# Gate products in a sequence of their own beside stick-breaking attention, with the adaptive visits gathered

## The chip, the cores and the metric

One core of a Trainium2 chip runs the whole program. The metric is the device time of one execution in microseconds (us). The engines work at the same time, each through its own instructions in order: TensorE (PE) does matrix products, ScalarE (ACT) and VectorE (DVE) work on elements, GpSimd (POOL) mostly issues DMAs here, SyncE (SP) issues the loads. They wait for each other by semaphores.

## The reference

One layer of a streaming encoder, for 1024 prompt rows and 32 sample rows of width 1024. What matters here:

```python
ada = silu(c) @ w_ada + b_ada            # 6 parts of 1024: shift, scale, gate, twice
h = rms_norm(x, g_pre_mix) * (1 + sc1) + sh1
p = h @ w_in                             # split: latents, rope key, SB q, k, v, gate A, gate B
...
# branch B: stick-breaking attention, 8 heads of 64, strictly causal
z = einsum('bqhd,bshd->bhqs', q, k) * SB_SCALE
sp = where(mask, softplus(z), 0.0)
later = cumsum(sp, reverse=True) - sp
a = where(mask, exp(log_sigmoid(z) - later), 0.0)
o_b = einsum('bhqs,bshd->bqhd', a, v)
...
merged = sigmoid(gate A) * (o_A @ w_proj_a) + sigmoid(gate B) * (o_B @ w_proj_b)
```

Then come an output projection, a residual with ada's gate, a convolutional feed-forward part of width 2816 and a second residual.

## The kernel before

The program runs its stages one after the other: `stage_h`, `stage_qkv`, `stage_sb`, `stage_lat`, `stage_mla`, `stage_merge`, `stage_up`, `stage_down`. The change lies in `stage_sb` (about 183 to 520 us of the profiled execution), and in what it calls.

`stage_sb` does the prompt's stick-breaking attention in four passes, one for each pair of heads. Beside it PE does two other things that nothing in the stage needs at once: the products of the two gates (`gates`), and a part of `ada` (`ada_step`).

Within a pass the order of PE, ACT and DVE is written out by hand: `sb_attend` goes through the list `ORDER`, and `manual_schedule` keeps that order on these three engines. SP and POOL are ordered by a scheduler. A token is a letter, then a query block of a head (0 to 7: head and a pair of 128 rows), then the tile or the key block, and a or b where a tile is done in two parts. The letters are:

- S: scores on PE (lines L1154, L1155). a, e, l: ACT takes the absolute value, exp and ln (L742, L744, L746). x: DVE makes softplus of it (L748). c: DVE's scan from the right, which is the cumulative sum (L755, L752); k copies the carry. d: DVE subtracts from the scores (L760). E: ACT takes exp (L762).
- T: PE transposes (L803). h and v: ACT and DVE split the transposed weights into a high and a low part (L68, L71). V: PE multiplies by the values (L817). o and p: ACT and DVE take the result out, and POOL stores it.
- f: one step of the gate products, three matmuls of 128x352 on PE (L75, L76, L77). G: ACT copies a finished gate bank to a "nat" buffer (L1080), and POOL stores it in `gd` (L1081). W and w: ACT and DVE split the next 128 columns of gate weights, which SP has loaded as `wr`, into high and low parts (L68, L71).
- D and Q: DVE adds a partial sum of `ada` (L244), or puts a finished part in place.

A gate tile `m` is 128 columns of `w_in`, done in three blocks of 352 rows and 8 steps each. There are 16 gate tiles, four to a pass. In the generator `steps`, behind the first block of each gate tile, stands a visit to `ada`: the products of two "A" tiles (128 rows of `w_ada` by 1024 columns) with the short matrix `cT`, each as 8 matmuls in the profile (L236); they take two f's of the list. `ada_step` also asks SP for the next two A tiles. So a pass has 96 f's for gates and 8 for ada. `stage_sb` asks for the first two A tiles ahead of the first head's V and of the weights of gate tile 1.

`stage_qkv` ends just before: it spills q, k and v to memory (`spill`, L478, by POOL), from where `queries` and `values` load them.

Of the kernel before, what the change touches and what calls it, by code (L numbers as in the profile page):

```python
# [8 lines left out]
F32 = mybir.dt.float32  # L9
# [35 lines left out]
class K:  # L45
# [182 lines left out]
    def ada_step(self, n, pool, tp, late):  # L228


        nc, a = self.nc, self.a
        ps = self.bank("mm")
        for i, (v, k) in enumerate(self.ada_todo[:n]):
            w = self.ada_w.pop(0)
            for j in range(4):
                nc.tensor.matmul(ps[32 * j : 32 * j + 32, :256], self.cT[:, k], w[:, j * 256 : j * 256 + 256],  # L236
                                 start=i == 0, stop=i == n - 1)
            if i < n - 1:
                yield
        if v > 2 and self.ada_todo[0][1] == 0:  # L240
            self.acc = self.tl(tp, [P, 256], F32, "ada")
            self.ada_bias(v)
        acc = self.acc
        late.append(lambda: nc.vector.tensor_tensor(acc, acc, ps[:, :256], ALU.add))  # L244
        del self.ada_todo[:n]
        self.ada_fetch(n, pool)
        self.ada_sum = v if k == KT - 1 else None
        yield

    def ada_turn(self):  # L250

# [192 lines left out]
    def stage_qkv(self):  # L444
# [245 lines left out]

    ORDER = """
        S0.0 S0.1 a0.0 S1.0 a0.1 e0.0 e0.1 l0.0 f2 l0.1 x0.0 a1.0 x0.1 f1 c0.1 c0.0 e1.0 f1 l1.0 f1 d0.0 d0.1
        E0.0 f1 x1.0 c1.0 E0.1 f1 S1.1 S2.0a a1.1 T0.0 d1.0 f1 G a2.0a h0.0 v0.0 f1 e2.0a f1 e1.1 S2.0b l2.0a D
        f2 l1.1 x2.0a V0.0 E1.0 c2.0a f1 a2.0b o0 f1 x1.1 e2.0b f1 W p0 f1 k2.0a d2.0a l2.0b f1 c1.1 E2.0a f1
        S2.1a x2.0b G f1 a2.1a d1.1 e2.1a c2.0b f2 E1.1 f1 w l2.1a S2.1b f1 a2.1b x2.1a T1.1 e2.1b T1.0 d2.0b
        h1.1 c2.1a f1 h1.0 f1 l2.1b v1.1 S3.0a E2.0b v1.0 f1 a3.0a f1 k2.1a d2.1a G e3.0a x2.1b V1.1 E2.1a c2.1b
# [3 lines left out]
        f2 x3.1b E3.1a f1 x4.0 c3.1b f1 G T3.3 c4.0 S4.1 a4.1 T3.2 h3.3 d3.1b f1 e4.1 v3.3 h3.2 f1 d4.0 f1 l4.1  # L700
        E3.1b v3.2 S5.0 f1 E4.0 x4.1 c4.1 a5.0 V3.3 e5.0 V3.2 l5.0 d4.1 T3.1 E4.1 x5.0 T3.0 h3.1 f1 c5.0 h3.0
        S5.1 S6.0a v3.1 a5.1 f1 v3.0 a6.0a T4.0 e5.1 f1 d5.0 h4.0 V3.1 E5.0 v4.0 f1 l5.1 V3.0 G x5.1 S6.0b e6.0a
        f1 o3 c5.1 f1 a6.0b l6.0a e6.0b f1 p3 l6.0b d5.1 f2 x6.0b E5.1 V4.0 x6.0a f1 o4 c6.0a S6.1a T5.1 p4
        a6.1a T5.0 k6.0a d6.0a h5.1 f1 c6.0b e6.1a f1 G h5.0 v5.1 f1 E6.0a v5.0 S6.1b l6.1a f1 W f1 x6.1a d6.0b
        V5.1 V5.0 D c6.1a E6.0b a6.1b S7.0a w o5 f2 e6.1b l6.1b a7.0a f1 k6.1a p5 e7.0a f1 d6.1a x6.1b E6.1a f1
        c6.1b l7.0a S7.0b f1 x7.0a T6.2 a7.0b f1 d6.1b h6.2 c7.0a f1 E6.1b f1 G e7.0b S7.1a v6.2 f1 k7.0a d7.0a
        l7.0b T6.1 T6.0 a7.1a h6.1 V6.2 x7.0b c7.0b h6.0 S7.1b e7.1a f1 v6.1 E7.0a f1 v6.0 l7.1a f1 d7.0b a7.1b
        f1 x7.1a V6.1 E7.0b V6.0 e7.1b c7.1a f1 G o6 l7.1b f1 p6 k7.1a d7.1a x7.1b f2 E7.1a f1 c7.1b f2 T7.3
        d7.1b T7.2 h7.3 f1 h7.2 E7.1b v7.3 f1 G f1 v7.2 f1 V7.3 V7.2 D T7.1 f1 h7.1 v7.1 T7.0 f1 h7.0 v7.0 f1
        V7.1 f2 V7.0 f1 o7 f1 W p7 f1 Q f1 w G f7 G  # L710
    """.split()

    def sb_attend(self, score, V, out, fill, then):
        nc = self.nc
        act, vec = nc.scalar.activation, nc.vector
        tiles, banks, seen = {}, {}, {}
        common = self.sums(V, out, tiles)
        todo = None
        for x in self.ORDER:
            if todo:  # L720
                todo()
            todo = then.get(x)
            k, x = x[0], x[1:]
            if k in "fGDQWw":
                for _ in range(int(x or 1)):
                    fill(k)
                continue
            h, u = divmod(int(x[0]), 4)
            if k in "SaelxckdE":
                n, i, part = x[0], int(x[2]), x[3:]  # L730
                w = (2 * u + i + 1) * P
                m = w // 2 if part else w
                c0 = m if part == "a" else 0
                if k == "S":
                    if part != "b":
                        tiles[x[:3]] = self.tl(self.At, [P, TP], F32, "A")
                    banks[x] = self.tl(self.ps, [P, 512], F32, "s")
                    score(h, banks[x], 2 * u + i, c0, max(m, 256))
                    continue
                ps, A = banks[x][:, :m], tiles[x[:3]][:, c0 : c0 + m]  # L740
                if k == "a":
                    act(A, ps, AF.Abs)  # L742
                elif k == "e":
                    act(A, A, AF.Exp, scale=-1.0)  # L744
                elif k == "l":
                    act(A, A, AF.Ln, bias=1.0)  # L746
                elif k == "x":
                    vec.scalar_tensor_tensor(A, ps, 0.0, A, ALU.max, ALU.add)  # L748
                elif k == "c":
                    r = A[:, ::-1]  # L750
                    if part == "b":
                        vec.tensor_tensor_scan(r, r, r, seen[x[:3]], ALU.add, ALU.bypass)  # L752
                    else:

                        vec.tensor_tensor_scan(r, self.reset[:, 512 - m : 512][:, ::-1], r, -NEG, ALU.mult, ALU.add)  # L755
                elif k == "k":
                    seen[x[:3]] = self.tl(self.sm, [P, 1], F32, "mn")
                    vec.tensor_copy(seen[x[:3]], A[:, 0:1])
                elif k == "d":
                    vec.tensor_tensor(A, ps, A, ALU.subtract)  # L760
                else:
                    act(A, A, AF.Exp)  # L762
                continue
            common(k, x, h, u)
# [278 lines left out]
    def gates(self):  # L1043
# [3 lines left out]
        w, ps, ada = [self.w_in_tile(2208)], [], []  # L1047
# [3 lines left out]
        def steps():  # L1051
            for m in range(16):
                wh, wl = w.pop(0)
                for b, (c0, n) in enumerate(self.BLK):
                    if b == 0:
                        c = 2208 + (m + 1) * P if m < 15 else 3 * P
                        raw.append(self.wload([(0, 1024, self.a["w_in"][0, :, c : c + P].rearrange("(k p) c -> p k c", p=P), 8)]))
                    ps.append((m, c0, n, self.bank("mm")))
                    for k in range(KT):
                        self.mm3(ps[-1][3][:, :n], wh[:, k], wl[:, k], self.Hh[k][:, c0 : c0 + n],  # L1060
                                 self.Hl[k][:, c0 : c0 + n], k == 0, k == KT - 1)
                        if k < KT - 1:
                            yield
                    if b == 1 and self.ada_sum is not None:
                        ada.append(self.ada_turn())
                    yield
                    if b == 0:
                        yield from self.ada_step(2, self.sm2, self.Sp, ada)
                        if m == 15:
                            self.sample_load(1)  # L1070

        step = steps()

        def do(kind):
            if kind == "f":
                next(step)
            elif kind == "G":
                m, c0, n, x = ps.pop(0)
                g = self.tl(self.At, [P, 512], F32, "nat")
                nc.scalar.copy(g[:, :n], x[:, :n])  # L1080
                nc.gpsimd.dma_start(self.gd[m, :, c0 : c0 + n], g[:, :n])  # L1081
# [24 lines left out]
    def stage_sb(self):  # L1106
# [35 lines left out]
            self.tl(S, [P, TP], F32, "A")  # L1142
        first(0)
        self.sm2 = self.tc.alloc_tile_pool(name="att", bufs=2, reuse_waits="tile")

        self.sent = self.wlast
        queries(0, 0)
        self.ada_w = []
        self.ada_fetch(2, S)
        values(0, 0)  # L1150

        def score(h, ps, i, c0, n):
# [2 lines left out]
            nc.tensor.matmul(ps[:, :n], Q[h][:, q], self.KLz[h][:, c0 : c0 + n], start=False, stop=True)  # L1155
# [1451 lines left out]
```

## Time and profile before

| | us |
|---|---|
| median of 3 runs (1705.19 to 1708.30) | 1707.84 |
| the profiled execution | 1706.82 |
| its span | 1704.7 |
| first score of pass 1 on PE | 193.01 |
| first score of pass 2 | 278.65 |
| first score of pass 3 | 358.06 |
| first score of pass 4 | 437.46 |

The granted clock of PE over the span is 0.994. In a row of a timeline stand the start in us from the span's start, the length in us, the engine, line and operation, the tile written and the tiles read, and the number of instructions; in square brackets is the engine's idle time ahead of it, with what released it. A matmul's start is exact, its end is modelled, so the start of the next one tells how long it held PE. In the table by stretches the brackets hold the number of instructions.

### The profile page before, as it was taken

The numbers are of one execution on the slowest core, as the hardware profiler recorded it, in microseconds if no ns is written. First come the engines' busy times: TensorE is split into PE (matmuls) and PEld (weight loads), VectorE is DVE, ScalarE is ACT, GpSimd is POOL, SyncE is SP. The second block draws the span as 40 slices with busy tenths as digits, with TensorE's granted clock in tenths as the row PEclk, the third lists the DMA queues.
The fourth block names the chain that finished last, engine by engine and source line by source line (L and its number), as shares of the span: only waits on it lengthen the run. The fifth ranks groups of instructions, "written<-read, shape, count | busy, mean of one in ns | idle before, by whom it ended". The sixth has DMA issues, their size and how long they took to land. (4 is left out here: it accounts for less than half of the span.)

```text
span 1704.7 us, 30268 instructions
## 1 busy us (share of the span) xinstructions
PE 1660.8 (97%) x11646; PEld 1512.1 (89%) x11646; DVE 1272.9 (75%) x2129; ACT 993.6 (58%) x1945; POOL 292.8 (17%) x569
## 2 busy tenths in 40 slices
PE   5999999999999999999999999999999999999997
PEld 3999889999999898998889789999999999887885
DVE  4865697979783688777766779887787777787456
ACT  4544597978774667777763476444444444544442
POOL 3113311111110221111100221221121111110013
PEclk8999999999999999999999999999999999999999
DMA  9345984647432421222374531433333333697643
GB/s 333 100 133 180 280 250 130 200 117 227 150 104 66 149 79 47 67 68 70 107 238 140 173 131 62 134 104 131 131 104 132 131 108 133 231 331 250 207 139 120
DMA packets 185728, 255.20 MB, mean 150 GB/s; under 512 B 14702, under 2 KB 125056, under 8 KB 185584
## 3 DMA queue, kind: packets, MB, share of 16 engines
q1 hardware_dynamic: 164944, 194.11, 36.5%
q0 software_dynamic: 20416, 59.08, 9.8%
q8 instruction: 91, 1.49, 0.4%
q14 instruction: 53, 0.43, 0.1%
q10 hardware_dynamic: 224, 0.09, 0.0%
HBM read 187.86 MB, written 64.57 MB: 148 GB/s over the span
## 5 line engine op out<-in xcount | busy, mean ns | idle before, releaser
L68 ACT ACTIVATE wh<-wr 128x1024 fp32r<-128x1024 f32 (+5 forms) x163 | 132.2, 820 | 226.3 <-PE s L2061 80.4
L71 DVE TENSOR_TENSOR wl<-wr,wh 128x1024 fp32r<-128x1024 f32 (+5 forms) x163 | 149.9, 928 | 78.0 <-ACT wh L68 77.6
L75 PE MATMUL mm<-hh,wh 128*128 128x352 f32 x456 | 153.0, 336 | 0.0
L76 PE MATMUL mm<-hl,wh 128*128 128x352 f32 x456 | 149.5, 328 | 0.4 <-DVE hl L331 0.3
L77 PE MATMUL mm<-hh,wl 128*128 128x352 f32 x456 | 148.7, 326 | 0.0
L2060 PE MATMUL mm<-T,wh 128*128 128x256 f32 (+1 forms) x376 | 108.1, 288 | 0.0
L2062 PE MATMUL mm<-T,wl 128*128 128x256 f32 (+1 forms) x376 | 107.0, 285 | 0.3 <-DVE wl L71 0.2
L2061 PE MATMUL mm<-T,wh 128*128 128x256 f32 (+1 forms) x376 | 106.7, 284 | 0.0
L2060 PE MATMUL s<-T,wh 128*128 128x256 f32 (+1 forms) x348 | 99.2, 285 | 0.0
L2062 PE MATMUL s<-T,wl 128*128 128x256 f32 (+1 forms) x348 | 99.1, 285 | 0.0
L2061 PE MATMUL s<-T,wh 128*128 128x256 f32 (+1 forms) x348 | 99.0, 284 | 0.0
L71 DVE TENSOR_TENSOR wl<-S,wh 128x1024 fp32r<-128x1024 f32 (+1 forms) x55 | 59.1, 1077 | 49.2 <-ACT wh L68 48.8
L76 PEld LDWEIGHTS mm<-hl,wh 128*128 128x128 f32 x456 | 86.4, 190 | 3.3 <-DVE hl L331 1.8
L75 PEld LDWEIGHTS mm<-hh,wh 128*128 128x128 f32 x456 | 86.4, 190 | 3.2 <-ACT A L762 1.6
L2201 DVE SCALAR_TENSOR_TENSOR u<-u,c,u 128x1058 f32<-128x1058 f32 x68 | 87.0, 1316 | 2.0 <-ACT u L2198 0.7
L77 PEld LDWEIGHTS mm<-hh,wl 128*128 128x128 f32 x456 | 86.5, 190 | 0.2
L803 PE MATMUL tr<-c,A 128*128 128x128 f32 x576 | 84.2, 275 | 0.9 <-DVE A L919 0.3
L68 ACT ACTIVATE wh<-S 128x1024 fp32r<-128x1024 f32 (+1 forms) x55 | 51.8, 943 | 49.5 <-PE s L2061 13.4
L2062 PE MATMUL tr<-T,wl 128*128 128x272 f32 (+1 forms) x272 | 77.6, 285 | 0.2 <-DVE wl L71 0.2
L2060 PE MATMUL tr<-T,wh 128*128 128x272 f32 (+1 forms) x272 | 77.7, 286 | 0.0
L2061 PE MATMUL tr<-T,wh 128*128 128x272 f32 (+1 forms) x272 | 77.3, 284 | 0.0
L71 DVE TENSOR_TENSOR PTl<-tr,PTh 128x512 fp32r<-128x512 f32 x96 | 64.5, 683 | 13.1 <-ACT PTh L68 12.3
(760 smaller groups left out, 5789.2 us busy)
## 6 DMA issues: line engine op xcount, KB each, us to landing
wr<-in_w_up_dram SPq DMA_DIRECT2D x44, 512.0 KB, 4.0
dr<-in_w_down_dram SPq DMA_DIRECT2D x43, 512.0 KB, 5.9
wr<-in_w_in_dram SPq DMA_DIRECT2D x33, 512.0 KB, 5.4
A<-in_w_ada_dram SPq DMA_DIRECT2D x32, 512.0 KB, 7.6
wr<-gdn SPq DMA_DIRECT2D x30, 512.0 KB, 5.0
gdn<-u POOLq DMA_DIRECT2D x23, 512.0 KB, 5.1
gd<-nat POOLq DMA_DIRECT2D x48, 176.0 KB, 4.1
t<-gd SPq DMA_DIRECT2D x16, 528.0 KB, 5.6
```

The costliest lines, as they stand in the source:

```text
L68: self.nc.scalar.activation(out, in_, AF.Identity, scale=scale)
L71: return self.nc.vector.tensor_tensor(out, full, hi.bitcast(F32), ALU.subtract)
L75: m(ps, lh, rh, start=start, stop=False)
L76: m(ps, lh, rl, start=False, stop=False)
L77: self.pe = m(ps, ll, rh, start=False, stop=stop).ins
L803: self.nc.tensor.transpose(tr[:, (2 * s + q) * P : (2 * s + q + 1) * P], at[q][:, b * P : b * P + P], self.idt)
L2060: m(ps[:, :n], w[0][:, k], x[0][:, k, c], start=first and k == 0, stop=False, skip_group_check=True)
L2061: m(ps[:, :n], w[0][:, k], x[1][:, k, c], start=False, stop=False, skip_group_check=True)
L2062: i = m(ps[:, :n], w[1][:, k], x[0][:, k, c], start=False, stop=k == 3, skip_group_check=True)
L2201: nc.vector.scalar_tensor_tensor(y, u[:, w : w + YW], self.cvT[:, w, cc : cc + 1], y, ALU.mult, ALU.add)
```

## The change

The gate work becomes a sequence of its own. `ORDER` keeps only f, 96 in a pass, at the places where gate steps stood; its other tokens stay as they are. G, W, w, D and Q move to a second list, `GATES`, which ties each to the number of the f behind which it comes, and which is gone through once for each pass. A new letter A in it is a visit of four A tiles, at f32 and f80 of a pass, in place of two tiles for each gate tile. `fill(LEAD)` does the first five f's ahead of the first pass, so ahead of its first scores; from there on every f of `ORDER` is the one five further along in `GATES`, and the last nine f's of the fourth pass find only four steps left.

The first four A tiles are loaded behind the second head's V of the first pass and lie in the pool `sm2`, whose buffers "big" and "A" are taken at once.

```diff
+LEAD = 5
...
     def ada_step(self, n, pool, tp, late):
                 nc.tensor.matmul(ps[32 * j : 32 * j + 32, :256], self.cT[:, k], w[:, j * 256 : j * 256 + 256],
                                  start=i == 0, stop=i == n - 1)
-            if i < n - 1:
-                yield
...
-        yield
...
     ORDER = """
         S0.0 S0.1 a0.0 S1.0 a0.1 e0.0 e0.1 l0.0 f2 l0.1 x0.0 a1.0 x0.1 f1 c0.1 c0.0 e1.0 f1 l1.0 f1 d0.0 d0.1
-        E0.0 f1 x1.0 c1.0 E0.1 f1 S1.1 S2.0a a1.1 T0.0 d1.0 f1 G a2.0a h0.0 v0.0 f1 e2.0a f1 e1.1 S2.0b l2.0a D
-        f2 l1.1 x2.0a V0.0 E1.0 c2.0a f1 a2.0b o0 f1 x1.1 e2.0b f1 W p0 f1 k2.0a d2.0a l2.0b f1 c1.1 E2.0a f1
-        S2.1a x2.0b G f1 a2.1a d1.1 e2.1a c2.0b f2 E1.1 f1 w l2.1a S2.1b f1 a2.1b x2.1a T1.1 e2.1b T1.0 d2.0b
...
-        l3.0a S3.0b V1.0 x3.0a a3.0b o1 f1 p1 T2.2 h2.2 e3.0b d2.1b f1 c3.0a f1 E2.1b f1 l3.0b v2.2 S3.1a k3.0a
-        d3.0a T2.1 h2.1 a3.1a x3.0b E3.0a V2.2 f1 c3.0b T2.0 e3.1a S3.1b h2.0 f1 v2.1 l3.1a f1 G v2.0 a3.1b f1
-        x3.1a W f1 d3.0b V2.1 c3.1a D V2.0 f1 w o2 S4.0 e3.1b E3.0b f1 a4.0 f1 l3.1b f1 p2 e4.0 k3.1a d3.1a l4.0
...
-        f1 o3 c5.1 f1 a6.0b l6.0a e6.0b f1 p3 l6.0b d5.1 f2 x6.0b E5.1 V4.0 x6.0a f1 o4 c6.0a S6.1a T5.1 p4
...
-        V7.1 f2 V7.0 f1 o7 f1 W p7 f1 Q f1 w G f7 G
+        E0.0 f1 x1.0 c1.0 E0.1 f1 S1.1 S2.0a a1.1 T0.0 d1.0 f1 a2.0a h0.0 v0.0 e2.0a e1.1 S2.0b l2.0a f2 l1.1
+        x2.0a V0.0 E1.0 c2.0a f1 a2.0b o0 f1 x1.1 e2.0b f1 p0 f1 k2.0a d2.0a l2.0b f1 c1.1 E2.0a f1 S2.1a x2.0b
+        f1 a2.1a d1.1 e2.1a c2.0b f2 E1.1 f1 l2.1a S2.1b f1 a2.1b x2.1a T1.1 e2.1b T1.0 d2.0b h1.1 c2.1a f1 h1.0
...
+        x3.0a a3.0b o1 f1 p1 T2.2 h2.2 e3.0b d2.1b f1 c3.0a f1 E2.1b f1 l3.0b v2.2 S3.1a k3.0a d3.0a T2.1 h2.1
+        a3.1a x3.0b E3.0a V2.2 f1 c3.0b T2.0 e3.1a S3.1b h2.0 f1 v2.1 l3.1a f1 v2.0 a3.1b x3.1a d3.0b V2.1 c3.1a
...
+        p3 l6.0b d5.1 f2 x6.0b E5.1 V4.0 x6.0a f1 o4 c6.0a S6.1a T5.1 p4 a6.1a T5.0 k6.0a d6.0a h5.1 f1 c6.0b
...
+        T7.1 f1 h7.1 v7.1 T7.0 f1 h7.0 v7.0 f1 V7.1 f2 V7.0 f1 o7 f1 p7 f9
+    """.split()
+
+    GATES = """
+        f9 G f4 W f4 G f3 w f5 G f7 A G f4 W f1 D f1 w f3 G f8 G f8 G W f1 w f8 G f7 G f7 A G f5 D f2 W f2 G w Q f7 G
     """.split()
...
     def gates(self):
                     yield
-                    if b == 0:
-                        yield from self.ada_step(2, self.sm2, self.Sp, ada)
-                        if m == 15:
-                            self.sample_load(1)
...
+            elif kind == "A":
+                self.ada_step(4, self.sm2, self.Sp, ada)
+                if not self.ada_todo:
+                    self.sample_load(1)
...
-        return do
+        parts = [[]]
+        for x in self.GATES * 4:
+            for _ in range(int(x[1:] or 1)):
+                if x[0] == "f":
+                    parts.append([])
+                parts[-1].append(x[0])
+        del parts[0]
+
+        def fill(n=1):
+            for _ in range(n):
+                for k in parts.pop(0) if parts else ():
+                    do(k)
+
+        return fill
...
     def stage_sb(self):
         self.sm2 = self.tc.alloc_tile_pool(name="att", bufs=2, reuse_waits="tile")
+        for g, w, n in (("big", BIG, 3), ("A", TP, 2)):
+            for _ in range(n):
+                self.tl(self.sm2, [P, w], F32, g)
...
         queries(0, 0)
-        self.ada_w = []
-        self.ada_fetch(2, S)
+        self.ada_w, self.ada_sum = [], None
         values(0, 0)
...
         fill = self.gates()
+        fill(LEAD)
         for p in range(4):
             then = {"S2.0a": lambda: queries(p, 1), "S2.1a": lambda: values(p, 1)}
+            if p == 0:
+                then["S2.1a"] = lambda: (values(p, 1), self.ada_fetch(4, self.sm2))
```

More of the change, by code (lines that the diff above doesn't have):

```diff
@@ L692 @@
         S0.0 S0.1 a0.0 S1.0 a0.1 e0.0 e0.1 l0.0 f2 l0.1 x0.0 a1.0 x0.1 f1 c0.1 c0.0 e1.0 f1 l1.0 f1 d0.0 d0.1
-        E0.0 f1 x1.0 c1.0 E0.1 f1 S1.1 S2.0a a1.1 T0.0 d1.0 f1 G a2.0a h0.0 v0.0 f1 e2.0a f1 e1.1 S2.0b l2.0a D
-        f2 l1.1 x2.0a V0.0 E1.0 c2.0a f1 a2.0b o0 f1 x1.1 e2.0b f1 W p0 f1 k2.0a d2.0a l2.0b f1 c1.1 E2.0a f1
-        S2.1a x2.0b G f1 a2.1a d1.1 e2.1a c2.0b f2 E1.1 f1 w l2.1a S2.1b f1 a2.1b x2.1a T1.1 e2.1b T1.0 d2.0b
-        h1.1 c2.1a f1 h1.0 f1 l2.1b v1.1 S3.0a E2.0b v1.0 f1 a3.0a f1 k2.1a d2.1a G e3.0a x2.1b V1.1 E2.1a c2.1b
@@ L702 @@
-        S5.1 S6.0a v3.1 a5.1 f1 v3.0 a6.0a T4.0 e5.1 f1 d5.0 h4.0 V3.1 E5.0 v4.0 f1 l5.1 V3.0 G x5.1 S6.0b e6.0a
-        f1 o3 c5.1 f1 a6.0b l6.0a e6.0b f1 p3 l6.0b d5.1 f2 x6.0b E5.1 V4.0 x6.0a f1 o4 c6.0a S6.1a T5.1 p4
-        a6.1a T5.0 k6.0a d6.0a h5.1 f1 c6.0b e6.1a f1 G h5.0 v5.1 f1 E6.0a v5.0 S6.1b l6.1a f1 W f1 x6.1a d6.0b
-        V5.1 V5.0 D c6.1a E6.0b a6.1b S7.0a w o5 f2 e6.1b l6.1b a7.0a f1 k6.1a p5 e7.0a f1 d6.1a x6.1b E6.1a f1
-        c6.1b l7.0a S7.0b f1 x7.0a T6.2 a7.0b f1 d6.1b h6.2 c7.0a f1 E6.1b f1 G e7.0b S7.1a v6.2 f1 k7.0a d7.0a
@@ new lines @@
+        f1 a2.1a d1.1 e2.1a c2.0b f2 E1.1 f1 l2.1a S2.1b f1 a2.1b x2.1a T1.1 e2.1b T1.0 d2.0b h1.1 c2.1a f1 h1.0
+        f1 l2.1b v1.1 S3.0a E2.0b v1.0 f1 a3.0a f1 k2.1a d2.1a e3.0a x2.1b V1.1 E2.1a c2.1b l3.0a S3.0b V1.0
+        x3.0a a3.0b o1 f1 p1 T2.2 h2.2 e3.0b d2.1b f1 c3.0a f1 E2.1b f1 l3.0b v2.2 S3.1a k3.0a d3.0a T2.1 h2.1
+        a3.1a x3.0b E3.0a V2.2 f1 c3.0b T2.0 e3.1a S3.1b h2.0 f1 v2.1 l3.1a f1 v2.0 a3.1b x3.1a d3.0b V2.1 c3.1a
+        V2.0 f1 o2 S4.0 e3.1b E3.0b f1 a4.0 f1 l3.1b f1 p2 e4.0 k3.1a d3.1a l4.0 f2 x3.1b E3.1a f1 x4.0 c3.1b f1
@@ new lines @@
+        T3.3 c4.0 S4.1 a4.1 T3.2 h3.3 d3.1b f1 e4.1 v3.3 h3.2 f1 d4.0 f1 l4.1 E3.1b v3.2 S5.0 f1 E4.0 x4.1 c4.1
+        a5.0 V3.3 e5.0 V3.2 l5.0 d4.1 T3.1 E4.1 x5.0 T3.0 h3.1 f1 c5.0 h3.0 S5.1 S6.0a v3.1 a5.1 f1 v3.0 a6.0a
+        T4.0 e5.1 f1 d5.0 h4.0 V3.1 E5.0 v4.0 f1 l5.1 V3.0 x5.1 S6.0b e6.0a f1 o3 c5.1 f1 a6.0b l6.0a e6.0b f1
+        p3 l6.0b d5.1 f2 x6.0b E5.1 V4.0 x6.0a f1 o4 c6.0a S6.1a T5.1 p4 a6.1a T5.0 k6.0a d6.0a h5.1 f1 c6.0b
+        e6.1a f1 h5.0 v5.1 E6.0a v5.0 S6.1b l6.1a f1 x6.1a d6.0b V5.1 V5.0 c6.1a E6.0b a6.1b S7.0a o5 f2 e6.1b
@@ new lines @@
+        l6.1b a7.0a f1 k6.1a p5 e7.0a f1 d6.1a x6.1b E6.1a f1 c6.1b l7.0a S7.0b f1 x7.0a T6.2 a7.0b f1 d6.1b
+        h6.2 c7.0a f1 E6.1b f1 e7.0b S7.1a v6.2 f1 k7.0a d7.0a l7.0b T6.1 T6.0 a7.1a h6.1 V6.2 x7.0b c7.0b h6.0
+        S7.1b e7.1a f1 v6.1 E7.0a f1 v6.0 l7.1a f1 d7.0b a7.1b f1 x7.1a V6.1 E7.0b V6.0 e7.1b c7.1a f1 o6 l7.1b
+        f1 p6 k7.1a d7.1a x7.1b f2 E7.1a f1 c7.1b f2 T7.3 d7.1b T7.2 h7.3 f1 h7.2 E7.1b v7.3 f1 v7.2 V7.3 V7.2
+        T7.1 f1 h7.1 v7.1 T7.0 f1 h7.0 v7.0 f1 V7.1 f2 V7.0 f1 o7 f1 p7 f9
@@ L723, in sb_attend @@
             k, x = x[0], x[1:]
-            if k in "fGDQWw":
+            if k == "f":
                 for _ in range(int(x or 1)):
-                    fill(k)
+                    fill()
                 continue
```

5 lines of the change are left out of this document (removed).

## The prediction, on record before the changed kernel ran

> **What bounds the kernel now.** I read the page first, then the table by stretches of 10 us over the stage that the change touches (about 183 to 520 us), then the timelines of each engine at its start and in its second pass.
>
> ```profile
> span 1704.7 us, 30268 instructions
> ...
> PE 1660.8 (97%) x11646; PEld 1512.1 (89%) x11646; DVE 1272.9 (75%) x2129; ACT 993.6 (58%) x1945; POOL 292.8 (17%) x569
> ```
>
> Over the program TensorE (PE) is full and VectorE (DVE) is not. By stretches it looks otherwise (columns: length, then busy time of PE, weight load, DVE, ScalarE (ACT), GpSimd (POOL), granted clock, DMA share, GB/s).
>
> ```profile
> 200.00:210.00 10.00, 10.00 (x63) 8.66 (x64) 6.89 (x13) 5.56 (x14) 4.84 (x10) 0.83 1.07 324
> ...
> 290.00:300.00 10.00, 9.66 (x65) 9.36 (x64) 9.93 (x17) 9.40 (x22) 1.26 (x4) 1.00 0.15 45
> 300.00:310.00 10.00, 10.00 (x76) 8.89 (x76) 9.90 (x18) 8.75 (x19) 1.54 (x3) 1.00 0.55 143
> ...
> 350.00:360.00 10.00, 10.00 (x68) 9.97 (x68) 2.85 (x6) 4.03 (x11) 3.67 (x7) 1.00 0.57 166
> ```
>
> In the middle of a pass (290 to 310) DVE is busy 9.9 of 10 us with the attention's own list; gate products fill PE. At a pass's end (350 to 360) DVE is nearly idle and PE alone sets the time. So in the middle, PE time saved is given back as waiting, while a delay of an ACT or DVE step that the list needs is kept. The first 20 us are a third regime: stalls, and 10 x (1 - 0.83) = 1.7 us of PE time lost to the clock.
>
> **The start of the stage.** PE's rows:
>
> ```profile
> 193.01 0.36 PE L1154 MATMUL s<-KH,Q 128*128 128x256 f32 x1
> ...
> 196.96 0.32 PE L76 MATMUL mm<-hl,wh 128*128 128x352 f32 x1
> 197.12 0.32 PE L77 MATMUL mm<-hh,wl 128*128 128x352 f32 x1
> 199.94 0.64 PE L1154 MATMUL s<-KH,Q 128*128 128x512 f32 x1 [2.49 <-DVE A L760]
> ...
> 201.34 0.85 PE L803 MATMUL tr<-c,A 128*128 128x128 f32 x3
> ...
> 202.99 1.29 PE L236 MATMUL mm<-A,cT 128*32 128x256 f32 x16
> ...
> 212.71 0.44 PE L1154 MATMUL s<-KH,Q 128*128 128x384 f32 x1 [1.36 <-DVE A L760]
> ```
>
> A matmul of a gate step starts 0.16 us after the one before (196.96, 197.12), so a step f of three is 0.48 us, and the five put ahead of the scores are 2.4 us. ACT's rows:
>
> ```profile
> 195.86 0.53 ACT L742 ACTIVATE A<-s 128x128 f32<-128x128 f32 x2
> ...
> 198.36 0.52 ACT L746 ACTIVATE A<-A 128x384 f32<-128x384 f32 x1
> 199.82 0.75 ACT L762 ACTIVATE A<-A 128x128 f32<-128x128 f32 x2 [0.94 <-DVE A L760]
> ...
> 203.10 0.45 ACT L1080 COPY nat<-mm 128x352 f32<-128x352 f32 x1 [0.44 <-PE mm L77]
> ...
> 210.12 1.06 ACT L68 ACTIVATE wh<-wr 128x1024 fp32r<-128x1024 f32 x1 [2.59 <-DMA wr<-in_w_in_dram]
> ...
> 217.15 0.46 ACT L1080 COPY nat<-mm 128x352 f32<-128x352 f32 x1
> ```
>
> *The lead.* ACT takes up the first scores only at 195.86, so scores that start at 193.01 + 2.4 = 195.4 hold it up by 0.2 at most. The lead's 2.4 us fall into the idle 2.49 ahead of 199.94: the second tile's score comes 0.25 earlier at most, not 2.49. What the lead earns is paid at the far end of the stage, where PE alone sets the time: of the last nine f's only four have work. **-2.4**.
>
> *The first weights.* The 2.59 that ACT waits for wr at 210.12, and the 1.36 on PE behind it, go: the two adaptive tiles (1 MB) no longer stand ahead of this load on SP's queue; their loads follow the second head's V instead. **-1.36**. The visit of 1.29 at 202.99, with 0.2 around it, goes from here: **-1.5**.
>
> *Two copies come too early.* GATES ties a gate tile's copy G (ACT) to the number of the f, and the lead moves the first, f9, from behind the first transposes to between e1.0 and l1.0, the row 198.36. The copy writes a "nat" buffer, whose memory was the source of the previous stage's spill qh<-T; the built program has the copy wait for that DMA. GpSimd's rows, and from the table of DMA issues the time to landing:
>
> ```profile
> 196.12 0.56 POOL L478 DMA_DIRECT2D qh<-T  x1 [1.53 <-ACT A L742]
> ...
> 208.11 0.57 POOL L1081 DMA_DIRECT2D gd<-nat  x1
> ```
>
> ```profile
> qh<-T POOLq DMA_DIRECT2D x1, 512.0 KB, 6.5
> ```
>
> ```profile
> gd<-nat POOLq DMA_DIRECT2D x1, 176.0 KB, 8.9
> ```
>
> The spill lands at 196.12 + 6.5 = 202.6; in before the copy ran at 203.10 and never felt it. Now ACT would stand at it from 198.4 to about 202.6, and ACT works in order: l1.0, E0.0, E0.1, a1.1, W, h0.0 queue behind. E0 (199.82 before) ends near 204, T0.0 near 204.3 in place of 201.34: **+3.0**, and PE, out of work at about 200.9, idles some 3.4 us. Bounds: 0 if the spill lands early (1 MB less in the queues) to +3.5. The clock loss of 1.7 then falls behind this gap instead of behind the 2.49: 0, or -1.7 if the gap shrinks. The third copy (f25) needs the first one's buffer back (two "nat" buffers). The first gd DMA is issued at 208.11, behind eight small bias loads on GpSimd's queue which the change leaves ahead of it, and lands at 217.0; before's third copy is at 217.15, just behind. Now ACT reaches it ahead of l2.1a, near 212.5: it waits 0 to 4.5. I take **+1.6**, since an earlier first copy can pull the issue forward by some of it, and DVE stood idle 2 us thereabouts. Start: -0.25 - 1.36 - 1.5 + 3.0 + 1.6 = **+1.5**, from -3.5 (T0.0 0.4 earlier, no waits) to +5.
>
> The Trainium skill, "TensorE: Matmul & The Clock Gate", Part 1, has the clock halve after an idle window of about 3.4 us; here 2.49 us of idle was enough for the stretch at 0.83, so the trace does not bear out that length. By that rule a gap of 3.4 stands at the edge; if it costs nothing, the sum is 1.7 lower.
>
> **A steady pass.** PE's rows of visits, then the steps around the moved ones:
>
> ```profile
> 284.25 0.32 PE L77 MATMUL mm<-hh,wl 128*128 128x352 f32 x1
> 284.50 1.07 PE L236 MATMUL mm<-A,cT 128*32 128x256 f32 x16
> 285.50 0.42 PE L1154 MATMUL s<-KH,Q 128*128 128x320 f32 x1
> 285.75 0.31 PE L1155 MATMUL s<-KL,Q 128*128 128x320 f32 x1
> ...
> 326.03 0.64 PE L236 MATMUL mm<-A,cT 128*32 128x256 f32 x8
> 326.60 0.44 PE L1154 MATMUL s<-KH,Q 128*128 128x384 f32 x1
> ```
>
> A visit of 16 matmuls lasts 1.00 (284.50 to 285.50), of 8 0.57: 0.43 per 8, so 0.14 of each is fixed. Going in costs 0.25 - 0.16 = 0.09, and the first product after it starts the next 0.25 later where about 0.15 would do, 0.1 more: 0.33 per visit. Before: four sites of two tiles a pass, one split by a score, so 20 visits; after: 8 of four tiles (1.00 + 0.86 + 0.2 = 2.05 each). PE saves 12 x 0.33 = 4.0 in all.
>
> ```profile
> 301.71 0.60 ACT L68 ACTIVATE PTh<-tr 128x512 fp32r<-128x512 f32 x1 [0.50 <-PE tr L803]
> ...
> 304.14 0.64 ACT L746 ACTIVATE A<-A 128x512 f32<-128x512 f32 x1
> ...
> 305.50 1.07 ACT L68 ACTIVATE wh<-wr 128x1024 fp32r<-128x1024 f32 x1
> ```
>
> ```profile
> 305.13 0.68 DVE L748 SCALAR_TENSOR_TENSOR A<-s,A 128x512 f32<-128x512 f32 x1
> ...
> 307.39 0.39 DVE L244 TENSOR_TENSOR ada<-ada,mm 128x256 f32<-128x256 f32 x1
> ...
> 322.17 0.67 DVE L760 TENSOR_TENSOR A<-s,A 128x512 f32<-128x512 f32 x1
> 322.84 0.89 DVE L748 SCALAR_TENSOR_TENSOR A<-s,A 128x320 f32<-128x320 f32 x2
> ```
>
> ```profile
> 322.34 0.47 ACT L746 ACTIVATE A<-A 128x320 f32<-128x320 f32 x1
> ...
> 327.75 1.06 ACT L68 ACTIVATE wh<-wr 128x1024 fp32r<-128x1024 f32 x1
> ```
>
> *The visit at f32* falls between T2.2 and S3.1a. There ACT already waits 0.50 for PE (h2.1, 301.71), so 2.0 more go through S3.1a, a3.1a, e3.1a to l3.1a; and W (1.06), behind it at 305.50 before, is tied to f36 and goes ahead of it. l3.1a is 3.06 late; x3.1a on DVE (305.13) started 0.35 after l3.1a's end (304.14 + 0.64), so DVE's list is 2.7 late, less one adaptive sum (0.39) that leaves: **+2.3**. *The split at f57/f58*: w stands on DVE right behind d5.1 (322.17 to 322.84), W on ACT behind l6.0b and a copy (0.45, as at 203.10): 322.34 + 0.47 + 0.45 + 1.06 = 324.3. DVE waits 324.3 - 322.84, less a little that successive ACT steps overlap: **1.4**, with x6.0b and the rest of the list queued behind w; W stood at 327.75 before, its w later. *The visit at f80* lies in the part that PE sets: 2.05 in place of the last pair's 1.19, **+0.8** at most. *The other pairs* free PE where it has slack: 0. The sum is +4.5 for a pass if nothing is caught up; if DVE had slack everywhere it would be PE's saving, -1.0. I take **+2.5** for each, towards the upper end because of the 9.9 of 10; for the shortfall, DVE idles that are there already swallow some. Four passes +10, from +4 to +16. The next pass's first score moves up among the last values of the pass before, an estimated -0.25 at three boundaries: **-0.8**.
>
> Sum: 1.5 - 2.4 + 10 - 0.8 = +8.3 on the profiled execution's 1706.82 (span 1704.7 and 2.1 around it): **1715.1**. The median of the runs, 1707.84, is 1.0 above that execution, a third of what counts as no change (0.2%, 3.4 us, about what a measurement of this kernel can tell from none).
>
> **The rivals.** *PE sets the time* (0.21). Then all PE time saved counts: 4.0 of visits, 2.2 of the idle before 199.94, 1.36 and 1.7: -9.3, **1697.5**. For it: PE 97% on the page, 10.00 in most stretches. Against: DVE 9.9 of 10 in the passes' middle, and ACT's wait at 301.71 for PE, which a longer visit lengthens. The Trainium skill, "Perfetto Trace Analysis", Identifying the Most-Contended Engine, would have the engine of highest occupancy (for PE its weight load, 89% here) worked on first, which is this rival; the trace bears it out for the stage's ends, not for its middle. *The waits cancel* (0.13): the spill lands early and the third copy waits little (start -2), lead and boundaries -3.2, and passes lose 1.2 each: -0.4, **1706.4**. *Slower by much* (0.12): DVE's wait at w is the mechanism, ending far later because wr for the split, now asked for in the busy queue after four 512 KB adaptive loads in a row, is not there. It decides once wr lands later than about 323 in each pass; at 5 us a pass in place of 2.5 the time is **1725**. My forecast has 0.54.
>
> Chances: slower 0.54 + 0.12 = 0.66, same 0.13, faster 0.21. The range takes in the rivals of both signs down to 1 in 10 on each side: 1698 to 1725; the forecast's own, by start and passes, is 1710 to 1722.
>
> **What would show it.** The first scores of passes 3 and 4 stand 79.4 us apart:
>
> ```profile
> 358.06 0.28 PE L1154 MATMUL s<-KH,Q 128*128 128x256 f32 x1
> ...
> 437.46 0.28 PE L1154 MATMUL s<-KH,Q 128*128 128x256 f32 x1
> ```
>
> In the changed profile: PE idle of 3 us or more before the first transposes, released by ACT, and the first copy near 202.6; the third copy waiting for a DMA; a DVE idle of 1 to 1.5 ahead of the second weight split of a pass, released by ACT; these first scores some 82 us apart; a last stretch 2.4 shorter. It is wrong if the first copy waits for nothing, if DVE runs through the split at f58, or if passes are no longer than before.

## The result, and the profile after

The changed kernel takes 1730.95 us in the median of four runs (1730.19 to 1732.04), the kernel before 1708.07 (four runs, 1705.19 to 1710.57). The ratio is 1.014, 95% interval 1.0126 to 1.0154. The forecast was 1715, with a range up to 1725: slower, as forecast, by nearly three times as much.

The profiled execution has a span of 1729.8 us, 25.1 more than before. The page of the changed kernel, its span and engines:

```profile
span 1729.8 us, 30239 instructions
...
PE 1664.4 (96%) x11646; PEld 1514.2 (88%) x11646; DVE 1272.8 (74%) x2121; ACT 992.7 (57%) x1945; POOL 295.4 (17%) x569
```

No engine has much more work: PE's busy time is up by 3.6 us, POOL's by 2.6, and DVE's and ACT's are not. The rest of the 25 us is waiting. The table by stretches shows it for one pass, from the second score of pass 3 to that of pass 4 (in the changed kernel the first score, at 362.05, has moved 10 us ahead of the second, among the values of the pass before). First the kernel before, then the changed one:

```profile
358.29:437.69 79.40, 78.80 (x556) 72.88 (x555) 67.53 (x118) 63.95 (x140) 11.00 (x20) 1.00 0.57 168
```

```profile
372.54:457.64 85.10, 80.10 (x556) 73.35 (x555) 67.34 (x116) 63.42 (x140) 10.99 (x20) 1.00 0.58 159
```

A pass is 5.7 longer. DVE has no more work, and PE is idle 5.0 us of it where it was idle 0.6; the other 1.3 is busy time of PE for the same number of matmuls.

To find the places I took the start of each instruction of the list in both traces (those of DVE and ACT whose order did not change) and subtracted. The difference is the lag of the changed kernel; where it steps, time is lost. An excerpt for pass 3, by token, with what stands at the step:

```
d1.0   363.86  378.02  +14.16
d2.0a  368.82  383.03  +14.21
c1.1   369.23  384.57  +15.34   w (f20) now stands ahead of it
d2.0b  373.71  388.70  +14.99
d3.0a  381.12  396.11  +14.99
E3.0a  382.14  399.18  +17.03   visit of four (f32) ahead of S3.1a
l3.1a  383.61  401.59  +17.98   W (f36) ahead of it
d3.0b  385.15  402.87  +17.71
d3.1a  388.76  406.15  +17.39   one adaptive sum less in between
d5.1   401.59  419.35  +17.75   a gate copy
c6.0a  403.18  422.99  +19.80   w (f58) waits for W (f57)
d6.1b  413.63  432.91  +19.28
d7.1b  424.99  444.23  +19.24
```

In pass 4 the same token d1.0 is 19.86 late. Net of the steps back, the pass loses 0.78 at f20, 2.40 at f32 to f38, 0.36 at a copy, 1.53 at f57/f58 and 0.62 at its end. Between the steps the lag is flat. It steps back, by 0.3 to 0.5, where a split or a sum has left that place of the list or where a short wait takes up some of it, so next to nothing is caught up. The gains at the far side are there too: over the whole stage the lag is +26.04 at the last values of pass 4 and +23.41 in the gate products behind them, so the lead is paid back by 2.6, as forecast (2.4).

For the first pass the same difference goes from -1.09 at the entry (earlier stages, which the change does not touch; it lay between -1.8 and +1.5 in the profiled runs of the experiments) to +3.44 at d3.0a, so the start costs 4.5. The timelines of ACT, then DVE, then PE:

```profile
196.88 0.53 ACT L745 ACTIVATE A<-A 128x384 f32<-128x384 f32 x1
204.33 0.45 ACT L1077 COPY nat<-mm 128x352 f32<-128x352 f32 x1 [6.92 <-DMA qh<-T]
204.68 0.53 ACT L747 ACTIVATE A<-A 128x384 f32<-128x384 f32 x1
...
206.08 1.06 ACT L69 ACTIVATE wh<-wr 128x1024 fp32r<-128x1024 f32 x1
...
217.00 0.45 ACT L1077 COPY nat<-mm 128x352 f32<-128x352 f32 x1 [1.13 <-DMA gd<-nat]
```

```profile
205.24 0.56 DVE L749 SCALAR_TENSOR_TENSOR A<-s,A 128x384 f32<-128x384 f32 x1 [6.20 <-ACT A L747]
```

```profile
205.76 0.90 PE L804 MATMUL tr<-c,A 128*128 128x128 f32 x3 [5.92 <-ACT A L763]
```

The first gate copy (L1077) holds ACT for 6.92 us until the spill qh<-T has landed. Behind it l1.0 (L747) is late; for that DVE idles 6.20, and PE idles 5.92 ahead of the first transposes. W (206.08) waits for nothing, as forecast. The third copy waits 1.13 for the first copy's store.

Inside pass 3, the visit and what hangs on it (ACT), and the split at f57/f58 (DVE):

```profile
398.20 0.60 ACT L69 ACTIVATE PTh<-tr 128x512 fp32r<-128x512 f32 x1 [2.22 <-PE tr L804]
...
400.64 1.07 ACT L69 ACTIVATE wh<-wr 128x1024 fp32r<-128x1024 f32 x1
401.59 0.64 ACT L747 ACTIVATE A<-A 128x512 f32<-128x512 f32 x1
```

```profile
419.35 0.67 DVE L761 TENSOR_TENSOR A<-s,A 128x512 f32<-128x512 f32 x1
420.93 1.23 DVE L72 TENSOR_TENSOR wl<-wr,wh 128x1024 fp32r<-128x1024 f32 x1 [0.91 <-ACT wh L69]
```

ACT waits 2.22 for PE where it waited 0.50 before, then does W, then l3.1a. DVE starts w 1.58 after d5.1, which itself lasts 0.67: 0.91 idle, and the 1.2 of w itself, stand ahead of the list at a place where w was not before.

### The profile page after: what moved, and what is told of

It is laid out like the page before. It is cut to its first block, busy times and chain, and to the rows that moved or that the text cites. A ratio compares the mean times of both kernels' runs of the same rounds, so it can differ in the third digit from the quotient of the medians.

```text
span 1729.8 us, 30239 instructions
## 1 busy us (share of the span) xinstructions
PE 1664.4 (96%) x11646; PEld 1514.2 (88%) x11646; DVE 1272.8 (74%) x2121; ACT 992.7 (57%) x1945; POOL 295.4 (17%) x569
## 5 line engine op out<-in xcount | busy, mean ns | idle before, releaser
L804 PEld LDWEIGHTS tr<-c,A 128*128 128x128 f32 x576 | 67.3, 141 | 17.2 <-ACT A L763 11.4
L749 DVE SCALAR_TENSOR_TENSOR A<-s,A 128x384 f32<-128x384 f32 (+4 forms) x96 | 52.0, 550 | 40.0 <-ACT A L747 39.6
L2079 PE MATMUL tr<-T,wh 128*128 128x272 f32 (+1 forms) x272 | 77.8, 286 | 0.0
```

The lines of the kernel that those rows point to most:

```text
L804: self.nc.tensor.transpose(tr[:, (2 * s + q) * P : (2 * s + q + 1) * P], at[q][:, b * P : b * P + P], self.idt)
L2079: m(ps[:, :n], w[0][:, k], x[0][:, k, c], start=first and k == 0, stop=False, skip_group_check=True)
```

## The experiments

The theory after the result: each loss is a token of GATES that stands at a place of ACT's, DVE's or PE's list where the list cannot spare it, at its own price (places). The rivals were that PE or the DMA queues set the time, or that the lead or the gathered visits cost by themselves. Pass lengths below are from the second score of pass 3 to that of pass 4: 79.40 before, 85.10 changed.

**The gate buffers moved.**

```diff
-... ("PTl", 512, 2), ("o", 256, 2), ("nat", 512, 2) ...
+... ("nat", 512, 2), ("o", 256, 2), ("PTl", 512, 2) ...
```

> The changed kernel with one edit: the two buffers for gate copies change places in the pool with PTl, so that the first copy no longer lands on the memory from which the previous stage's last spill is read. Theory (places: each loss is a token of GATES that stands too early in ACT's or DVE's list, at its own price): the 6.9 us wait of ACT at the first copy goes, T0.0 comes near 200.5 in place of 207, but ACT then meets the third copy sooner, whose buffer comes free only when the first gd DMA has landed (near 217), so 4 to 5 us of it come back there; net 0 to -5, 1728 likeliest. Rival (the start is late because the loads and spills crowd the queues, not because of this buffer): some other wait takes its place before T0.0 and the time stays at 1731.

Measured: 1734.45 us (ratio to before 1.0165, 1.015 to 1.018), 3.5 more than the changed kernel, where the theory had 0 to 5 less. ACT's timeline of this kernel:

```profile
198.62 0.43 ACT L1077 COPY nat<-mm 128x352 f32<-128x352 f32 x1
...
218.12 0.45 ACT L1077 COPY nat<-mm 128x352 f32<-128x352 f32 x1 [6.53 <-DMA gd<-nat]
```

The first copy waits for nothing, so the buffer was the cause of that wait, and the first transposes come at 200.98. But ACT now runs into the third copy, which holds it for 6.53 us: the wait that had cost 1.13 was hidden behind the first. The theory's mechanism holds, its price (4 to 5) was too low: from the entry to d3.0a the start costs 5.3 in place of 4.5. The rest of the 3.5 us is not settled. This profile has three stretches of 3.41 us at half clock, at 258.6, 429.3 and 569.2, that the changed kernel's has not, and its four runs have a mean granted clock of 0.989 to 0.990 against 0.992 to 0.994.

**Three buffers for gate copies**, on the other memory.

```diff
+... ("nat", 512, 3) ...
+self.tl(self.At, [P, 512], F32, "nat", 3)
```

> The changed kernel with three buffers for gate copies in place of two, on memory that the previous stage's last spill does not read, so that neither the first copy waits for the spill nor the third for the first gd DMA. Theory (the two waits stand in series, and taking away the first alone only moved ACT on to the second): both go, pass 1 reaches its fourth block (d3.0a) 4.5 us sooner against its entry than the changed kernel, 1726 (1724 to 1728). Rival (the start is late for the crowd in the DMA queues): a third wait appears and the time stays at 1731 or above.

Measured: 1727.15 us (1.0125, 1.011 to 1.0141), within the theory's range. Both waits are gone; ACT's first and third copies in this kernel:

```profile
199.70 0.43 ACT L1077 COPY nat<-mm 128x352 f32<-128x352 f32 x1
...
212.14 0.43 ACT L1077 COPY nat<-mm 128x352 f32<-128x352 f32 x1
```

The lag from entry to d3.0a is -2.7 instead of +4.5, so the two waits together cost 7.2 there (with the loss of clock that follows them), and without them the start would have been a gain. Over the whole kernel the medians differ by 3.8; the entry of this profiled run was 2.4 later than that of the changed kernel's, and I cannot say how much of the rest is chance.

**No lead.**

```diff
-LEAD = 5
+LEAD = 0
```

> The changed kernel with LEAD = 0 in place of 5 and nothing else. GATES keeps its numbers, so each of its tokens comes five f's later in the attention's list. Theory (places): the visit of four falls behind l3.1a in place of ahead of S3.1a (+0.9 for a pass against before, not +2.05), W at f57 and w at f58 come where before had them, the first copy comes after the spill has landed; the lead's 2.5 at the end of the stage is lost. Passes near 80 us, time 1704 to 1710. Rival (PE sets the time, and the visits of four or the loads are what costs): the lead was a gain of 2.5 us, so without it 1733.

Measured: 1713.56 us (1.0043, 1.0028 to 1.0058), passes of 80.55. Most of the loss goes by shifting every token five f's later, so the rival falls; but it is 3.5 us above the theory's range. The trace names the remainder: W at f36 and w at f38 now stand behind one another right in the list, and DVE waits for ACT.

```profile
392.37 0.41 DVE L243 TENSOR_TENSOR ada<-ada,mm 128x256 f32<-128x256 f32 x1
394.02 1.22 DVE L72 TENSOR_TENSOR wl<-wr,wh 128x1024 fp32r<-128x1024 f32 x1 [1.24 <-ACT wh L69]
```

I had priced W and w at f57/f58 and not looked at the other pair. The start, too, keeps a wait of 3.7 us for a copy's buffer.

**The splits put back.**

```diff
-... A G f4 W f1 D f1 w f3 G f8 G f8 G W f1 w f8 G ...
+... A G f6 D W f1 w f2 G f8 G f8 G f5 W f2 w f2 G ...
```

> The changed kernel with only the second and third weight splits of a pass put back to the places in the list that they had before (W from f36 to f38, w from f38 to f39, the adaptive sum from f37 to f38; W from f57 to f62, w from f58 to f64). Theory (places): the 0.95 that l3.1a loses behind W and the 1.5 that DVE waits for W ahead of x6.0b go, 2.5 us a pass, 10 in all: 1721. Rival (the splits only fill waits that PE imposes): the waits move elsewhere and the time stays within 2 us of 1731.

Measured: 1721.47 us (1.0086, 1.0069 to 1.0103), passes of 82.41, that is 2.7 less. DVE's timeline at the same place of pass 3 runs through:

```profile
414.20 0.67 DVE L761 TENSOR_TENSOR A<-s,A 128x512 f32<-128x512 f32 x1
414.80 0.87 DVE L749 SCALAR_TENSOR_TENSOR A<-s,A 128x320 f32<-128x320 f32 x2
```

This is what the prices said, 9.5 of the 23 us.

**Visits of two again**, at f16, f40, f64 and f80, and the lead kept.

```diff
-f9 G f4 W f4 G f3 w f5 G f7 A G f4 W f1 D f1 w f3 G f8 G f8 G W f1 w f8 G f7 G f7 A G f5 D ...
+f9 G f4 W f3 A G f4 w f1 D f4 G f7 G f4 W f2 w f2 A G f5 D f4 G f8 G W f1 w f6 A G f5 D f4 G f7 A G f5 D ...
-                self.ada_step(4, self.sm2, self.Sp, ada)
+                self.ada_step(2, self.sm2, self.Sp, ada)
...
-                then["S2.1a"] = lambda: (values(p, 1), self.ada_fetch(4, self.sm2))
+                then["S0.1"] = lambda: self.ada_fetch(2, self.sm2)
```

> The changed kernel with four visits of two A tiles for each pass (f16, f40, f64, f80, their copies at the same f, their sums five f's on) in place of two visits of four (f32, f80); the first two A tiles are asked for early in the first pass, behind its first scores. Everything else, the lead too, stays. Theory (places): S3.1a is no longer 2.05 late, the end of a pass gains 0.6, the new places cost little since PE has slack there: -2 for a pass, near 1723. Rival (gathering saves PE time that counts): eight more visits at 0.33 make it 1734.

Measured: 1728.88 us (1.0131, 1.0116 to 1.0147), between the two; passes are 85.26. The step of 2.05 at S3.1a is gone, but the lag now steps by 1.2 at f40, where the changed kernel's steps by 0.4, and by 1.3 between c6.0a and d6.1b, where the changed kernel's falls by 0.5. The visit of f64 stands in that stretch, but so does a loss of clock. PE waits 1.6 us for DVE behind w (f58) in both kernels, and here the clock is halved after it for 3.41 us, in every pass. Two neighbouring stretches of 3.41 us from pass 3, first of this kernel, then of the changed one:

```profile
421.32:424.73 3.41, 1.79 (x10) 1.42 (x10) 3.31 (x7) 1.18 (x3) 0.54 (x1) 1.00 1.06 365
424.73:428.14 3.41, 3.41 (x14) 3.16 (x12) 2.96 (x7) 1.21 (x3) 0.43 (x1) 0.50 0.33 128
```

```profile
421.36:424.77 3.41, 2.06 (x14) 1.67 (x13) 3.28 (x7) 2.19 (x6) 0.20 (x1) 1.00 1.06 330
424.77:428.18 3.41, 2.89 (x15) 2.35 (x16) 3.41 (x7) 1.35 (x4) 0.34 (x1) 1.00 0.13 35
```

At half clock PE loses 1.7 us, nearly the whole difference of 1.8 between the two kernels' steps. So what the visit of f64 costs by itself, and whether PE has slack there, is not shown.

**One visit moved**, from f32 to f40.

```diff
-... f7 A G f4 W f1 D f1 w f3 G f8 ...
+... f7 G f4 W f2 w f2 A G f5 D f4 G f8 ...
```

> The changed kernel with only the first visit of each pass moved from f32 to f40, its copy and its sum with it (the copy from f41 to f40, the sum from f37 to f45). Theory of places: S3.1a is no longer 2.05 late, and f40 was near a place where before hid a visit of two, so about 1.2 of the 2.05 is saved, -5 in all: 1726. Rival (a block of 2.05 is longer than any wait of PE there, so it costs its length at either place): passes stay at 85 us, 1731.

Measured: 1733.0 us (1.0149, 1.0126 to 1.0171), passes of 85.24. Inside the pass the rival is nearly right: the step at S3.1a is 0, and one of 2.06 stands between d3.1a and d5.1, where the changed kernel has 0.36 for a copy. So the move saves 2.06 at one place and costs 1.7 at the other. The whole pass says less: passes 2 to 4 have 3.41 us at half clock here too (in pass 3 from 428.40), and the end of pass 3 costs 1.3 in place of 0.6.

**Products left out, in the kernel before and in the changed one.** In the first, one of the two A tiles of each visit is left out, in the second three of the four; neither computes all of `ada`.

```diff
-            for j in range(4):
+            for j in range(4) if i else ():          # before;  "if i == n - 1" in the changed kernel
...
-                                 start=i == 0, stop=i == n - 1)
+                                 start=True, stop=True)
```

> The kernel before, with the products of one of the two A tiles of every adaptive visit left out: 16 times 0.43 = 6.9 us less PE time, all else in place. If PE has slack in the middle of a pass, as the prediction's step said, only the visits at the ends count and the time falls by about 2 (1705 to 1706). If PE sets the time everywhere it falls by 7 (1700).

> The changed kernel with the products of three of the four A tiles of each visit left out, so that a visit lasts 0.75 in place of 2.05; all else in place. In the kernel before, half of the products left out gave 0.4 us a pass. Theory (the gathered visit of f32 stands in the list's way for its length, that of f80 at the end too): 1.3 at each of the two, -2.6 a pass, 82.5 us, 1720. Rival (DVE's list sets the pass and hides the visits, the loss is the splits' and copies' alone): -0.4 a pass, 1729.

Measured: 1705.34 (0.9986, 0.9976 to 0.9997) and 1724.96 (1.0106, 1.009 to 1.0123). In the kernel before a pass falls by 0.39, to 79.01, although PE has four times 0.43 less to do: the lag stays within 0.03 through the pass and falls by 0.4 at its end. So shortening three of its four visits gains nothing, and only the one at the end counts. The table by stretches of that kernel, for the same pass:

```profile
355.40:434.41 79.01, 77.48 (x524) 72.03 (x523) 67.43 (x118) 63.73 (x140) 11.00 (x20) 1.00 0.57 170
```

PE's busy time falls by 1.32 and its idle time rises by 0.93. In the changed kernel leaving products out gives 1.7 a pass (83.44): the step at S3.1a shrinks from 2.05 to 1.15 and that at the end goes. This pass, unlike the changed kernel's, has 3.41 us at half clock (from 420.95). Between d3.0a of pass 2 and d3.0a of pass 3, without such a loss in either kernel, the gain is 2.05 (83.05 in place of 85.10). So the gathered visit is not hidden. At 1.7 to 2.05 for 2.6 of PE time it costs somewhat less than its length, and the theory's 2.6 was too much.

**The places of before, with a lead of four.** Every G, W and w at before's place or the next f; visits of four at f40 and f80; three buffers.

```diff
+f12 G f5 W f3 G f4 w f4 G f8 G f1 W f1 w f2 A G f5 D f7 G f8 G f1 W f1 w f8 G f6 G f4 A G f5 D f6 W f1 Q f1 G w f3 G
```

> The changed kernel with LEAD = 4 and a GATES list that puts every G, W and w at the place in the attention's list that it had before, or at the next f behind it, visits of four at f40 and f80, and the three buffers of the run beside it. With a lead of 4 the weights of the next gate tile need not be ready before the place that the split had. Theory (places): each price of the changed kernel's passes goes but the visit's (0.9 more at f40, 1.2 less at each of two places); passes 79 to 80 us, the lead's 2 us and the start's 2 to 3 are kept: 1702 (1698 to 1708). Rival (the lead or the gathering itself costs): passes stay at 83 us or more, 1718 and above.

Measured: 1708.95 us (1.0014, 1.0005 to 1.0024; ten runs, before 25 runs at 1707.14). Passes are 80.79. With the tokens where they were, 22 of the 23 us are gone, lead and gathering and all. About 7 of them lie at the start, where the three buffers act (d3.0a comes 3.0 earlier against the entry than before, in the changed kernel 4.5 later), the rest in the passes. But the hoped-for gain on before is not there. The lag of a pass steps by 2.0 at f40 and by 0.6 at the end, the two visits, and falls back by 1.2 elsewhere.

**The first visit at the end of the pass before** (f8, passes 2 to 4), all else as in that kernel.

> The kernel of the run beside it, with the first visit of passes 2 to 4 moved from f40 to f8, into the stretch between two passes in which DVE is nearly idle. Theory (a visit in the middle of a pass delays the list by its length, one in the stretch that PE sets costs its PE time alone): 1 to 2 us less for each of three passes, 1698 (1694 to 1703). Rival (a visit costs its length wherever it stands): no difference from the run beside it.

Measured: 1708.10 us (1.001, 0.9999 to 1.002), passes of 80.81, as beside it. Against each other the two kernels show what the visit costs at each place: from d1.0 to d2.0a the lag steps by +1.2 with it and by -0.5 without, from d3.1a to d5.1 by +2.0 with it and by +0.3 without, so 1.7 at f8 and 1.7 at f40. Between these two places the rival, for which the place makes no difference, is right.

**Visits at before's own places, of two and of four** (lead of four, three buffers).

```diff
+two:  f12 G A f4 G f1 W D f7 w f4 G f8 G A f1 W f1 D w f2 G f12 G f8 G A f1 W f1 D w f2 G f12 G f8 G A f1 D ...
+four: f12 G f5 W f3 G f4 w f4 G f8 G A f1 W f1 D w f2 G f12 G f8 G f1 W f1 w f8 G f6 G f8 G A f1 D ...
```

> As the kernel with the places restored (LEAD = 4, three buffers), but with visits of two A tiles at the four places of the attention's list that before had (f12, f36, f60, f84, in the middle of a block, with the copies of four blocks some f's sooner to free the banks), the first two tiles asked for behind the first scores. Theory (a visit is free only where PE would wait anyway, and before had its visits at such places: half of their products left out gave 0.4 us a pass): passes near before's 79.4, lead and start keep 3 to 5 us, 1703 (1700 to 1706). Rival (the sequence itself, with its lead, costs 1.4 us a pass wherever the visits stand): 1709 again.

> As the run beside it, but with visits of four at two of before's places (f36 and f84) and none at f12 and f60. Theory (the place decides, not the number of visits): at f36 0.9 more than before had there, at f84 about 0.9 more of PE time with 0.4 saved on entries, the other two places were free and give nothing: passes 80 to 80.5, 1706 (1703 to 1709). Rival (gathering saves PE time that counts): passes 78.5, 1699.

Measured: 1718.94 (1.0069, 1.0054 to 1.0084) and 1709.84 (1.0012, 1.0004 to 1.0021). The first is spoilt by its start. PE's timeline of it:

```profile
210.75 1.08 PE L237 MATMUL mm<-A,cT 128*32 128x256 f32 x8 [7.91 <-DMA A<-in_w_ada_dram]
...
213.01 1.08 PE L237 MATMUL mm<-A,cT 128*32 128x256 f32 x8 [1.18 <-DMA A<-in_w_ada_dram]
```

PE waits 9.1 us for the first A tiles. Its passes are 80.34, 0.45 less than with visits of four at f40 and f80, those of the second 81.32. So with the lead gathered visits, in part at other places, cost 0.5 to 1.0 a pass more than visits of two. But visits of two do not reach 79.40 either: their lag rises by 2.0 from d1.0 to d7.1b and falls by 1.1 behind it. Which of the differences from before costs the remaining 0.94 (the lead, the copies that come sooner, the first scores of a pass that move up by some 10 us) is not shown. No kernel that computes all of `ada` beat the one before.

## Why the prediction was right or wrong

The direction and most of the mechanisms were right. The step that failed is the last one of the pass: "The sum is +4.5 for a pass if nothing is caught up ... I take +2.5 for each ... DVE idles that are there already swallow some." The items that it had were of the right size; the discount of 2.0 a pass was wrong, and items of 1.1 a pass were missing.

| term of the forecast | forecast | measured |
|---|---|---|
| visit at f32 and W at f36, per pass | +2.3 | +2.40 |
| split at f57/f58 | +1.4 | +1.53 |
| visit at f80 | +0.8 at most | +0.62 |
| split at f20, a copy | not seen | +0.78, +0.36 |
| sum of a pass | +4.5, taken as +2.5 | +5.7 |
| start, to d3.0a | +1.5 (-3.5 to +5) | +4.5 |
| lead at the end | -2.4 | -2.6 |
| next pass's first score earlier | -0.8 in all | none seen apart from the visit at f80 |

Four passes at 5.7 in place of 2.5 are 12.8 us, the start 3.0 and the scores 0.8: 16.6. The forecast's +8.3 with these is 24.9; the spans differ by 25.1. An entry 1.1 earlier and 1.7 more in the later stages (23.4 to 25.1), which the change does not touch, nearly cancel.

*The pass.* DVE's idle time in the kernel before, 79.40 - 67.53 = 11.9 us a pass, is of no use to the list. From d1.0 to d7.1b DVE idles 2.8, and ahead of an instruction it waits more than 0.15 at three places only (0.82, 0.35, 0.45), two of them ahead of the split at f20. The other 9.0 lies behind d7.1b, where PE sets the time and has a full list of its own (10.00 of 10 in the forecast's row of 350 to 360). In the table by stretches of the kernel before, these two parts of pass 3:

```profile
363.86:424.99 61.13, 60.53 (x425) 55.76 (x425) 58.29 (x100) 54.86 (x120) 8.76 (x16) 1.00 0.56 165
424.99:443.26 18.27, 18.27 (x132) 17.12 (x130) 9.24 (x19) 9.09 (x21) 2.21 (x4) 1.00 0.67 202
```

So a lag from the middle is carried through the end, flat, into the next pass. The two terms that I missed have the same cause as those that I saw: with a lead of five the split that the sixth f needs must stand earlier in DVE's list (without the lead the step at f20 is absent), and I followed only the moves at f36 and f57.

*The start.* The first copy's wait for the spill was forecast, with 4.2 at most; it took 6.92, since the spill needed longer to land. From the table of DMA issues of the changed kernel:

```profile
qh<-T POOLq DMA_DIRECT2D x1, 512.0 KB, 9.1
```

That is 9.1 in place of 6.5 for the same 512 KB. The bound from before's row was not one: it came from a queue with other loads in it. The third copy's wait came as forecast (1.13 for 1.6), and the run with moved buffers shows that its full size is 6.5. By the run with three buffers both together cost 7.2, and the rest of the start is a gain of 2.7, where I had -3.5.

*The clock.* The loss fell behind the new gap, as forecast, and was a little larger. In the table by single microseconds of the changed kernel (the number after POOL's is the granted clock) PE stops at 199.84 and starts again at 205.76:

```profile
202.00:203.00 1.00, 0.00 (x0) 0.00 (x0) 0.00 (x0) 0.00 (x0) 0.94 (x2) 0.95 1.04 422
203.00:204.00 1.00, 0.00 (x0) 0.00 (x0) 0.00 (x0) 0.00 (x0) 0.00 (x0) 0.50 1.03 422
...
209.00:210.00 1.00, 1.00 (x6) 1.00 (x6) 0.85 (x2) 1.00 (x4) 1.00 (x3) 0.63 0.89 176
210.00:211.00 1.00, 1.00 (x9) 1.00 (x9) 1.00 (x3) 0.72 (x4) 0.09 (x1) 1.00 0.95 260
```

The clock halves some 3.1 us after the last product and comes back at 209.7, some 4.0 us after the first: half of that is lost, 2.0, where the kernel before lost 1.7. The Trainium skill, "TensorE: Matmul & The Clock Gate", Part 1, gives about 3.4 us for both; in this trace neither time is that, and in the kernel before a gap of 2.5 was enough.

*The rivals.* PE does not set the time of the whole pass: in the kernel before, 1.7 us of products left out gave 0.39. The rival "slower by much" had the right mechanism, DVE's wait at w, but not its reason: W itself is late in ACT's list, so that DVE idles 0.91, and W waits for no load.

*The sign of the visits.* The forecast put the saved entries at 0, and that was right in its sign: shortening three of before's four visits gained nothing, so the 4.0 us were not there to gain. What it did not say is why. Blocks of 2.05 were free nowhere that was tried (2.05 at f32, 1.7 to 2.05 at f40, 1.7 at f8, 0.6 at f80). That blocks of about 1.2 fit the waits that PE has in the list at before's places is the likely reason; the runs show only that 0.43 of each is free there.

## What to carry to other kernels

When every step of a delay has been followed to the engine that is full, take the sum as it stands: slack on an average, or elsewhere in the loop, does not give a lag back, and only a wait that lies on the same chain does. A small piece can lie, in part at least, in a wait that is there anyway (0.43 us less in each of three visits gained nothing); gathering such pieces then saves entries that cost little and makes a block that must be paid for (0.5 to 1.0 us a pass with the tokens at before's places). Before a pass length is put down to an edit, look at the granted clock in it: in two runs here a loss of 1.7 us of PE time in every pass, or nearly every one, stood beside the effect asked for. Where a wait is taken away, look for the next one in the same engine's order: here two waits on one engine stood in series, and removing the first alone gave the second its full length.

## What the runs showed of the hardware

The same spill of 512 KB took 6.5 us to land in one kernel and 9.1 in the other, with the DMA engines full (share about 1.0) in both. In the changed kernel SP had issued the second head's loads of q and k by 193.8, ahead of the spill (195.03); in the kernel before the last of them followed at 201.85, behind the spill (196.12). That these loads made the difference is likely, not shown. A landing time from one trace was no bound for another order of the loads. The entry of the stage, behind 190 us that no edit touched, moved by up to 3.3 us between profiled executions (-1.8 to +1.5 against before's), nearly the size of the effects asked for; differences inside the stage had to be taken from its own entry.

The halved clock comes in stretches of 3.41 us or a multiple of it (the one that ends with the program aside). Cut each of the fourteen traces into windows of 3.41 us along the edges of these stretches. Between 190 and 540 us every window in which PE was idle for 0.48 or more of it is followed by one at half clock, and no window idle for 0.47 or less is. This is inferred from these traces alone; behind 540 us, in the next stage, two windows with only 0.17 idle were followed by half clock, so idle time is not all that counts. By it a gap of 1.6 us is enough when it falls into one window (1.62 of 3.41 idle with visits of two) and does nothing when an edge divides it (1.35 and 0.52 in the changed kernel). So the same wait costs the clock in one kernel and not in another.
